# A gated MLP's gate and up projections by seven block products over pairs of token chunks, pairs outermost

## Chip, cores and metric

One core of one Trainium2 chip. The metric is the device time of one execution in microseconds (us). Engines: PE (TensorE matmul), PEld (its weight load), DVE (VectorE), ACT (ScalarE), POOL (GpSimd), SP (SyncE, which here only issues transfers).

## The reference, cut to what the change touches

One layer of a decoder on 2048 tokens of width 1024, in float32: a first projection, four sequence mixers (RWKV, mLSTM, sliding window, "fox" attention with forget gates), an output projection, and a gated MLP with a short convolution. The change is in how the last lines are computed:

```python
x = x + _rmsnorm(y @ w_out[l], norm_mix_post[l])
h = _rmsnorm(x, norm_ffn_pre[l])
gate, up = jnp.split(h @ ffn_w_up[l], 2, axis=-1)     # 1024 -> 2 x 2816
gate = _causal_dwconv(gate, ffn_conv_w[l], ffn_conv_b[l])   # 3 taps over time
f = jax.nn.gelu(gate, approximate=True) * up
x = x + _rmsnorm(f @ ffn_w_down[l], norm_ffn_post[l])
```

## The kernel before, in words

Every large product is made of float16 parts: an operand x becomes hi = float16(x s) and lo = float16(x s - hi) with a power of two s, and a product is three matmuls, hi hi + hi lo + lo hi, into one psum bank.

Stage 1 (RWKV and the windowed mixers) fills the first 1,200 us. Stage 2 runs the fox attention and, between its steps, the **output projection** by tiles of 128 tokens, the "o tiles". `o_front` loads a tile of y, scales it and transposes it by DMA into `yt` (L289); `o_back` multiplies it with the resident `Wo` (L275 to L277: 96 matmuls of 256 columns), norms it, adds x, writes the result to DRAM (`x2`), and `norm_u` puts the normed tile as hi/lo, again through DMA transposes, into `U2`: four resident tiles `V` of 512 tokens each, which the MLP reads. All transposes, and the loads of y and of the weights, go through SP's queue in program order.

Stage 3, `stage_n`, is the MLP (the "mixer"). The 2816 channels are 22 blocks of 128 (j), taken in 11 groups (g) of two. Groups are the outer loop, the four chunks (c) of 512 tokens the inner one. Once per group `split_w` prepares the weights: load to `wst` (L232), absolute maximum per row on DVE (L233), over the partitions on POOL (`partition_all_reduce`, L238), hi on ACT (L252), lo on DVE (L253). Then for each chunk:

```python
for jj in range(GF):                       # two channel blocks
    self.gemm_cm(pg, w, U[c], 0)           # gate: 24 matmuls of 512 columns
    ...gb = [two old columns | gate], 3 taps on DVE (L1489 to L1491), gelu on ACT (L1492)
    self.gemm_cm(pu, w, U[c], P)           # up: 24 matmuls
    f = pu * un * t                        # DVE, L1496
nc.gpsimd.partition_all_reduce(...)        # L1500: one scale for the float16 parts of f
...fh, fl on ACT and DVE (L1507, L1508)
for i in range(NSUB): for n in range(2):   # down: 48 matmuls into psd, acc += on DVE (L1522)
```

In the mixer POOL has only copies and memsets of two columns (L1482, L1484, L1487) and the two reductions (L238, L1500). In the last group each finished tile goes through the last norm: DVE L1531, a POOL addition of 128x1024 (L1532), the write to `out`. Small powers (`rsqrt`) are a POOL tensor_tensor too (L215). The order on each engine is made by a scheduler from the program; pools of one or two buffers set what may run ahead.

Of the kernel before, what the change touches and what calls it, by code (L numbers as in the profile page):

```python
# [31 lines left out]
# ---------------------------------------------------------------- constants of the shapes  # L32
# [65 lines left out]
def _layout(inp):  # L98
    """Only moves the inputs about."""
# [18 lines left out]
    up = a["ffn_w_up"].reshape(KT, P, 2, NF, P).transpose(3, 1, 0, 2, 4)  # L118
# [20 lines left out]
# ---------------------------------------------------------------- the program  # L139
class Trunk:  # L140
# [13 lines left out]
    # ---- set-up  # L154
    def setup(self):
# [16 lines left out]
        # norm gains brought to [-2, 2) by a power of two, which the output's scale undoes  # L172
        self.gsc = cst.tile([P, 2], F32, name="gsc")
        self.ug = cst.tile([P, 2], F32, name="ug")
        for n, k in enumerate(("g1", "g2")):
            m = self.small.tile([P, 1], F32, name="gm")
            nc.vector.tensor_reduce(out=m, in_=self.pc[k], axis=AX.X, op=ALU.max, apply_absolute_value=True)
            mm = self.small.tile([P, 1], F32, name="gmm")
            nc.gpsimd.partition_all_reduce(mm, m, P, RMAX)
            un, sc = self.pow2(mm, 0)  # L180
            nc.vector.tensor_copy(out=self.gsc[:, n:n + 1], in_=sc)
            nc.vector.tensor_scalar(out=self.ug[:, n:n + 1], in0=un, scalar1=2.0 ** -9, scalar2=None, op0=ALU.mult)
# [17 lines left out]
    def pow2(self, m, e):  # L200
        """(un, sc): un = 2**(exponent of m) * 2**-e, sc = 1 / un."""
        nc = self.nc
        o = self.small.tile([P, 3], F32, name="p2")
        nc.vector.tensor_scalar(out=o[:, 0:1], in0=m, scalar1=1e-30, scalar2=2.0 ** -e, op0=ALU.max, op1=ALU.mult)
        nc.vector.tensor_scalar(out=o[:, 1:2].bitcast(I32), in0=o[:, 0:1].bitcast(I32), scalar1=0x7F800000, scalar2=None, op0=ALU.bitwise_and)
        nc.vector.reciprocal(out=o[:, 2:3], in_=o[:, 1:2])
        return o[:, 1:2], o[:, 2:3]

    def rsqrt(self, out, v, mul, eps):
        """out = (v * mul + eps) ** -0.5, on small tiles."""  # L210
# [6 lines left out]
    def sigm(self, e):  # L217
        """e = 1 / (1 + e), by ScalarE's exp and ln."""
# [5 lines left out]
    def split_w(self, pool, tag, srcs, n, ug, bufs=None):  # L224
        """Loads [P, n] weights (given as pieces; with self.twice, again for each use), returns hi, lo (float16) of w * sc and the undoing scale."""
# [31 lines left out]
    def gemm_cm(self, ps, w, u, n0=0, nn=P, step=C):  # L257
        """ps[n, t] = sum_d w[d, n] u[d, t], in steps over t"""
# [10 lines left out]
    def gemm_tm(self, ps, u, sl, w, n0, nn):  # L269
        """ps[t, n] = sum_d u[d, t] w[d, n]"""  # L270
# [8 lines left out]
    def split_t(self, x, sc, h, out):  # L279
        """hi/lo float16 parts of the token tile x * sc (sc per token, or None), channel-major."""  # L280
# [10 lines left out]
    def norm_u(self, pool, x, n, grow, U, i, h=None, bufs=1):  # L291
        """Normalises the token tile x (in place) and puts it channel-major, as hi/lo float16 scaled by 2**9, into slice i of U."""
# [29 lines left out]
    # ---- stage 1: first norm, RWKV-7, and the input projection of the other groups  # L322
    def stage1(self):
# [8 lines left out]
        with ExitStack() as cx:  # L332
# [46 lines left out]
    def rwkv_setup(self, xp):  # L379
# [18 lines left out]
        # block-diagonal tiles with a background of zeros  # L398
# [15 lines left out]
    def rwkv_mix(self, c, j, w, cy):  # L414
        """Channel-major projection j of chunk c with the token shift mixed in, to DRAM."""
# [30 lines left out]
    def rwkv_unit(self, c, hp, half):  # L446
        """Two heads, 256 tokens: four chunks of 64, two token tiles of 128."""
# [21 lines left out]
        # decay  # L469
# [12 lines left out]
        # a  # L482
# [5 lines left out]
        # normalised kk  # L488
# [11 lines left out]
        # scaled forms; bk has (beta, k) for even and (k, beta) for odd chunks  # L500
# [16 lines left out]
        # gate and bonus (with the norm's offset)  # L517
# [21 lines left out]
        # token-major, after M^T: BK = [beta~; k~] (odd chunks the other way round), V opposite to where U will be, alpha^  # L539
# [9 lines left out]
        # M^T, entry [s, t]: rows (beta, k) as in bk, columns (alpha, r)  # L549
# [39 lines left out]
        # merge 16 -> 32; F1, F2 the parts of M between 16-blocks of a 32-block and between 32-blocks; items (h, i)  # L589
# [20 lines left out]
        # X = M_ak V  # L610
# [9 lines left out]
        # [W | U] = T64 [alpha^ | X], T64 = T32 + T32 F2 T32  # L620
# [16 lines left out]
        # chunk operators  # L637
# [18 lines left out]
        # chain of states  # L656
# [13 lines left out]
        # outputs  # L670
# [9 lines left out]
        # per-head layer norm, bonus, gate  # L680
# [15 lines left out]
    # ---- projections of the other groups, to DRAM  # L696
    def fillers(self, ctx):
# [43 lines left out]
        # forgetting attention's queries (negated) and keys as sums of two float32r parts  # L741
# [50 lines left out]
        # values as two float16 parts: head, [hi | lo]. The operands' scales bound the sums by 2**35.  # L792
# [68 lines left out]
    # ---- stage 2: mLSTM, sliding-window and forgetting attention, output projection  # L861
    def stage2(self):
        with ExitStack() as ck, ExitStack() as co:
# [14 lines left out]
            with ExitStack() as cf:  # L878
                self.fox_pools(cf, 5, 6, 8, 4, 2, 4)
                self.u2p = self.pool(self.ctx, "u2", side="right")  # L880
# [4 lines left out]
                for c in range(1, NC):  # L885
                    if c > 1:
                        self.fox(8)
                    if c <= 2:
                        self.o_tiles(c - 1)
            ck.close()  # L890
            u2b = self.pool(self.ctx, "u2b")
            for c in range(2, NC):
                self.U2[c] = u2b.tile([P, 2, KT, C], F16, name=f"V{c}")
            for c in range(2, NC):
                self.o_tiles(c)

    def logsig(self, pool, x, name):
        """log sigmoid of a small tile"""
# [9 lines left out]
    def gates_f(self, kp, psp):  # L908
        """Cumulative sum of the forgetting attention's log gates, as two float32r parts, to DRAM."""
# [29 lines left out]
    def gates_m(self, kp, tp, psp):  # L939
        """All gates of mLSTM at once; blocks of 128 tokens lie on partitions 16 * head + block."""  # L940
# [26 lines left out]
        # the running maximum across the blocks  # L967
# [25 lines left out]
        # token-major: g, weights, exp(-m)  # L993
# [10 lines left out]
        # rows to broadcast by the tensor engine, as two float32r parts below each other  # L1004
# [11 lines left out]
    def gates(self, ctx):  # L1016
        """The gates of mLSTM and of the forgetting attention, the sliding window's bias."""
# [21 lines left out]
    def mlstm_front(self, ib):  # L1039
        """What does not wait for the state: q times exp(a), k with its weights, the decay matrix."""  # L1040
# [10 lines left out]
        # q times exp(a), broadcast over the channels of each head; k token-major with its weights  # L1051
# [9 lines left out]
        # decay matrix exp(a_t + g_s), s <= t  # L1061
# [9 lines left out]
    def mlstm_back(self, ib, q, k, va, so, qi, kw, Dm):  # L1071
# [13 lines left out]
        # state, block-diagonal over the heads  # L1085
# [7 lines left out]
        # h = num / max(|den|, exp(-m)), its norm, output gate  # L1093
# [16 lines left out]
    def swa_bias(self, tp):  # L1110
        """Rows of the relative bias with the window's mask, to DRAM, from where they are read with a shift per partition."""
# [60 lines left out]
            # numerators as two float16 parts, keys on the partitions  # L1172
# [41 lines left out]
    # forgetting attention; its logits, negated, have float32 operands as sums of two float32r parts  # L1214
# [7 lines left out]
    def fox_setup(self):  # L1222
# [9 lines left out]
        # values as two float16 parts: tile of tokens, head, [hi | lo]  # L1232
# [139 lines left out]
    def o_tiles(self, c):  # L1372
        if c == 0:
            self.of = self.o_front(0)
# [191 lines left out]
```

## Time and profile before

| | us |
|---|---|
| median of three runs (lowest, highest) | 3163.35 (3162.02, 3165.93) |
| the profiled execution: span of the instructions | 3156.8 |
| what the median has beyond this span | 6.5 |
| to 1200: stage 1; 1200 to 1640: fox phase with 11 of the 16 o tiles | 1640 |
| 1640 to 1785: the other five o tiles, and the first mixer matmuls | 145 |
| 1785 to 3111: mixer | 1326 |
| 3111 to the end: last norms and writes | 46 |

A row by stretches has the busy time of each engine in that stretch with its count of instructions, then the granted clock of PE (1.00 is 2.4 GHz, 0.5 is 1.2 GHz), the share of the 16 DMA engines and their rate. A timeline row has start, duration, engine, line, operation, tiles and shapes, and in brackets how long the engine was idle before it and what ended that; "issue" stands for nothing that the profile shows.

### The profile page before, as it was taken

What the parts mean: (1) busy time and instruction counts of PE and PEld (TensorE: products, weight loads), DVE (VectorE), ACT (ScalarE), POOL (GpSimd) and SP (SyncE); (2) the same over time, 40 slices, a digit from 0 to 9 for tenths busy, and PEclk for the clock granted to TensorE, in tenths of its full rate; (3) what the DMA queues carried; (4) which work ended last, traced back from release to release, by engine and by line L of the source; (5) the groups of instructions that cost most, each with busy time, mean ns of one, the idle gap of its engine ahead of it and who ended that gap; (6) DMA issues with size and microseconds to landing.
All of it is one profiled execution on the core that took longest, in us unless ns stands there. A gap on an engine that the chain in (4) does not pass through costs nothing. (4 is left out here: it accounts for less than half of the span.)

```text
span 3156.8 us, 45312 instructions
## 1 busy us (share of the span) xinstructions
PE 2793.4 (88%) x17006; PEld 1665.4 (53%) x17006; DVE 1899.9 (60%) x4341; ACT 963.9 (31%) x2004; POOL 586.2 (19%) x943
## 2 busy tenths in 40 slices
PE   1599889898997998787777899999999999999995
PEld 0145577676776876575554444444444444444442
DVE  3474555557775665677765455655655656556565
ACT  2342222335542234566653211211111211111121
POOL 1243222222322332122221100000000000000033
PEclk9799889899997998688888899999999999999998
DMA  6442323244653378999985200100100100001023
GB/s 177 100 111 60 93 57 96 81 104 117 153 137 86 83 196 186 241 213 220 190 194 134 67 27 14 41 14 27 41 14 27 40 13 28 27 14 40 14 99 115
DMA packets 460580, 291.47 MB, mean 92 GB/s; under 512 B 351736, under 2 KB 407416, under 8 KB 460360
## 3 DMA queue, kind: packets, MB, share of 16 engines
q1 hardware_dynamic: 396704, 236.34, 30.1%
q10 hardware_dynamic: 63656, 52.23, 6.1%
q8 instruction: 134, 2.20, 0.3%
q14 instruction: 86, 0.70, 0.1%
HBM read 153.10 MB, written 66.43 MB: 70 GB/s over the span
## 5 line engine op out<-in xcount | busy, mean ns | idle before, releaser
L1522 DVE SCALAR_TENSOR_TENSOR acc<-psd,uns,acc 128x512 f32<-128x512 f32 x320 | 237.0, 749 | 210.9 <-PE psd L1518 209.6
L1516 PE MATMUL psd<-hi_dn,fh 128*128 128x512 f16 x704 | 268.6, 382 | 17.7 <-ACT fh L1507 17.5
L1517 PE MATMUL psd<-lo_dn,fh 128*128 128x512 f16 x704 | 268.8, 382 | 0.0
L265 PE MATMUL psg<-V,hi_up 128*128 128x512 f16 x704 | 267.1, 379 | 0.0
L267 PE MATMUL psg<-V,lo_up 128*128 128x512 f16 x704 | 266.8, 379 | 0.1
L266 PE MATMUL psg<-V,hi_up 128*128 128x512 f16 x704 | 266.8, 379 | 0.0
L265 PE MATMUL psu<-V,hi_up 128*128 128x512 f16 x704 | 266.8, 379 | 0.0
L266 PE MATMUL psu<-V,hi_up 128*128 128x512 f16 x704 | 266.8, 379 | 0.0
L267 PE MATMUL psu<-V,lo_up 128*128 128x512 f16 x704 | 266.8, 379 | 0.0
L1518 PE MATMUL psd<-hi_dn,fl 128*128 128x512 f16 x704 | 261.7, 381 | 0.3
L267 PEld LDWEIGHTS <-lo_up 128*128 128x128 f16 x1408 | 137.8, 98 | 166.3 <-DVE lo_up L253 0.6
L265 PEld LDWEIGHTS <-hi_up 128*128 128x128 f16 x1408 | 137.8, 98 | 165.7
L266 PEld LDWEIGHTS <-hi_up 128*128 128x128 f16 x1408 | 137.8, 98 | 165.6
L275 PE MATMUL psg<-Wo,yt 128*128 128x256 f16 x512 | 149.3, 292 | 54.2 <-DMA yt<-hl 54.2
L1485 ACT ACTIVATE gb<-psg,un_up 128x512 f32<-128x512 f32 x88 | 60.3, 686 | 386.7 <-PE psg L267 386.7
L265 PE MATMUL psg<-U,hi_cm 128*128 128x512 f16 x256 | 104.3, 407 | 70.9 <-ACT hi_cm L252 70.9
L233 DVE TENSOR_REDUCE wm<-wst 128x1 f32<-128x1024 f32 (+1 forms) x91 | 109.6, 1206 | 92.4 <-DMA wst<-in_w_up 51.2
L265 PE MATMUL psf<-U,hi_fm 128*128 128x256 f16 x576 | 162.2, 282 | 1.9 <-DVE zf L745 1.9
L1487 POOL COPY gtail<-gb 128x2 f32<-128x2 f32 x88 | 18.8, 214 | 775.5 <-ACT gb L1485 775.5
L266 PE MATMUL psf<-U,hi_fm 128*128 128x256 f16 x576 | 162.3, 282 | 0.0
L267 PE MATMUL psf<-U,lo_fm 128*128 128x256 f16 x576 | 162.1, 281 | 0.0
L276 PE MATMUL psg<-Wo,yt 128*128 128x256 f16 x512 | 148.9, 291 | 0.0
(423 smaller groups left out, 6291.3 us busy)
## 6 DMA issues: line engine op xcount, KB each, us to landing
wst<-in_w_up SPq DMA_DIRECT2D x44, 512.0 KB
wst<-in_w_dn SPq DMA_DIRECT2D x22, 512.0 KB
zin<-zR SPq DMA_DIRECT2D x80, 128.0 KB
ka<-kA ACTq DMA_DIRECT2D x40, 256.0 KB
wst<-in_w_cm SPq DMA_DIRECT2D x17, 512.0 KB
zR<-m SPq DMA_DIRECT2D x32, 256.0 KB
wso<-in_w_o SPq DMA_DIRECT2D x32, 256.0 KB
xr<-in_x ACTq DMA_DIRECT2D x16, 512.0 KB
```

The lines of the kernel that those rows point to most:

```text
L233: nc.vector.tensor_reduce(out=m[:, i:i + 1], in_=st[:, :w], axis=AX.X, op=ALU.max, apply_absolute_value=True)
L265: nc.tensor.matmul(ps[:, sl], lhsT=hi[:, k, n0:n0 + nn], rhs=uh[:, k, sl], start=k == 0, stop=False)
L266: nc.tensor.matmul(ps[:, sl], lhsT=hi[:, k, n0:n0 + nn], rhs=ul[:, k, sl], start=False, stop=False)
L267: nc.tensor.matmul(ps[:, sl], lhsT=lo[:, k, n0:n0 + nn], rhs=uh[:, k, sl], start=False, stop=k == KT - 1)
L275: nc.tensor.matmul(ps, lhsT=uh[:, k, sl], rhs=hi[:, k, n0:n0 + nn], start=k == 0, stop=False)
L276: nc.tensor.matmul(ps, lhsT=uh[:, k, sl], rhs=lo[:, k, n0:n0 + nn], start=False, stop=False)
L1485: nc.scalar.activation(out=gb[:, 2:], in_=pg, func=AF.Copy, scale=un)
L1487: nc.gpsimd.tensor_copy(out=prev[jj], in_=gb[:, C:C + 2])
L1516: nc.tensor.matmul(ps, lhsT=fh[:, jj, sl], rhs=dh[:, o], start=jj == 0, stop=False)
L1517: nc.tensor.matmul(ps, lhsT=fh[:, jj, sl], rhs=dl[:, o], start=False, stop=False)
L1518: nc.tensor.matmul(ps, lhsT=fl[:, jj, sl], rhs=dh[:, o], start=False, stop=jj == GF - 1)
L1522: nc.vector.scalar_tensor_tensor(out=acc[t][:, ns], in0=ps, scalar=uns, in1=acc[t][:, ns], op0=ALU.mult, op1=ALU.add)
```

## The change

**Products.** Let a pair be two chunks, and split the 1024 inputs of a product into two halves of 512. Gate and up of one block j over a pair are then a 2x2 by 2x2 block product, which is done with seven products instead of eight (Winograd's form). Each has K = 512: 12 matmuls of 512 columns, so 84 per j and pair instead of 96. The operands are sums of weight quarters (three more per j, `S`) and of input quarters (three more, and a fourth as step between). The seven go into three psum banks a, b, c, one buffer each, and are put together by ACT and DVE.

**Order.** Pairs are outermost: pass 0 does all 11 groups for the first pair, pass 1 for the second. In pass 0 the prepared weights (seven quarters hi and lo) are also written to DRAM (`wU`, `wD`), from where pass 1 loads them back.

**Inputs.** An o tile and the one 512 tokens later are combined (`o_combine`), transposed (28 blocks of 128x128 each for hi and lo) and written to DRAM (`u2d`, 7.3 MB per pair); `load_u(p)` brings a pair back in seven loads of 1 MB, once before the second pair's o tiles, and once between the passes.

The core of the diff:

```diff
+    def o_combine(self, p, i, q):
+        tt = lambda o, x, y: nc.vector.tensor_tensor(out=q[:, o], in0=q[:, x], in1=q[:, y], op=ALU.subtract)
+        nc.gpsimd.tensor_tensor(out=q[:, 4], in0=q[:, 1], in1=q[:, 0], op=ALU.subtract)
+        tt(2, 0, 6)
+        tt(3, 1, 2)
+        tt(5, 7, 3)
...
+        nc.scalar.copy(out=h[:, 0], in_=qv)
+        nc.sync.dma_start_transpose(out=ut[:, 0]..., in_=h[:, 0])
+        nc.vector.tensor_tensor(out=h[:, 1], in0=qv, in1=h[:, 0], op=ALU.subtract)
+        nc.sync.dma_start_transpose(out=ut[:, 1]..., in_=h[:, 1])
+        for n in range(2):
+            nc.sync.dma_start(out=dst, in_=ut[:, n])
...
-            for g in range(NG):
-                    Wt.append(self.split_w(self.wp, "up", [a[0], a[1]], 2048, self.ug[:, 1:2], bufs=3))
-                for c in range(NC):
+            for p in range(2):
+                if p:
+                    self.load_u(p)
+                for g in range(NG):
+                    for jj in range(GF):
+                        self.ffn_up(p, j, self.up_weights(p, j), F[:, jj], m[:, jj], prev)
+                    Wd = self.down_weights(p, g, GF)
+                    prev = self.ffn_down(p, g, GF, NG, F, m, Wd, acc)
...
+    def up_weights(self, p, j):
+        if p:
+            nc.sync.dma_start(out=W..., in_=self.wU[j])
+            return W
+        nc.sync.dma_start(out=R..., in_=self.A["w_up"][j])            # L1522, 1 MB
+        nc.vector.tensor_reduce(out=m[:, 0:1], in_=R..., op=ALU.max, apply_absolute_value=True)
+        nc.gpsimd.partition_all_reduce(m[:, 1:2], m[:, 0:1], P, RMAX)  # L1525
+        gt = lambda o, x, y, op: nc.gpsimd.tensor_tensor(out=o, in0=x, in1=y, op=op)   # L1529
+        gt(S[:, 1], R[:, 2], R[:, 0], ALU.subtract)
+        gt(R[:, 0], R[:, 0], R[:, 1], ALU.add)
+        gt(S[:, 0], R[:, 0], R[:, 2], ALU.subtract)
+        gt(S[:, 2], R[:, 3], S[:, 0], ALU.subtract)
+        for o, x in ((slice(0, 4), R), (slice(4, 7), S)):
+            nc.scalar.activation(out=W[:, 0, o], in_=x, func=AF.Copy, scale=sc)
+            nc.vector.scalar_tensor_tensor(out=W[:, 1, o], in0=x, scalar=sc, in1=W[:, 0, o], op0=ALU.mult, op1=ALU.subtract)
+        nc.sync.dma_start(out=self.wU[j], in_=W...)
...
+    def ffn_up(self, p, j, W, F, m, filler):
+        product(a, 2, 5, True, False)          # 12 matmuls each, then next(filler): one psd tile of the group before
+        nc.scalar.activation(out=X, in_=a, func=AF.Copy, scale=un)
+        product(b, 4, 2, True, False)
+        add(g2, b, X)
+        product(a, 3, 6, False, True)
+        product(b, 5, 3, False, False)
+        product(c, 0, 1, True, False)
+        product(b, 1, 4, False, True)
+        product(c, 6, 0, False, True)
...
+        nc.gpsimd.tensor_tensor(out=t, in0=t, in1=up..., op=ALU.mult)  # L1607, 128x1024
+    def ffn_down(...):
+        nc.gpsimd.partition_all_reduce(mm[:, 2:4], mm[:, 0:2], P, RMAX)  # L1615
...
+                elif t % 2 and n:
+                    nc.scalar.activation(out=tmp, in_=ps, func=AF.Copy, scale=us)
+                    nc.gpsimd.tensor_tensor(out=acc[t][:, ns], in0=tmp, in1=acc[t][:, ns], op=ALU.add)  # L1639
```

The taps now run on both chunks at once (1024 columns), one on ACT and two on DVE. `down_weights` is like `split_w` (reduction at L1552) with a write to `wD` in pass 0, a load in pass 1. The last norm (`ffn_out`, L1650 to L1658) is as before, with its tile of x in the pool of the raw weights (two buffers). The other hunks of the diff drop comments and renumber lines.

**POOL, steady mixer.** First a stretch of the kernel before (`gtail` and `gb`: the two columns carried between chunks; `wmm`, `fm`: the maxima of weights and of f); a row "ISA" that names tiles is a reduction:

```order
L238 ISA wmm<-wm 128x1
L1484 COPY gb<-gtail 128x2
L1487 COPY gtail<-gb 128x2
L1484 COPY gb<-gtail 128x2
L1500 ISA fm<-fm 128x1
```

Then one half of a group in pass 0 of the changed kernel. A bare "ISA" row, without tiles, is an instruction that sets up POOL's code for the row behind it:

```order
L1525 ISA
L1525 ISA wm<-wm 128x1
L1529 ISA
L1529 TENSOR_TENSOR raw<-raw 128x512
L1615 ISA
L1615 ISA fmm<-fmm 128x2
L1529 ISA
L1529 TENSOR_TENSOR S<-raw 128x512
L1529 TENSOR_TENSOR S<-raw,S 128x512
L1525 ISA
L1525 ISA wm<-wm 128x1
L1601 COPY tails<-gb 128x2
```

Additions and reductions now alternate; the steady mixer had no bare row before. In pass 0 there are 83 of them, in pass 1 there are 21; the whole program has 150 against 62.

**SP, from the last o tiles to the first weights.** Before, the loads of weights (`wst`) stand between the transposes of the last o tiles:

```order
L289 DMA_TRANSPOSE V_17300<-hl 128x8x128 x2
L1408 DMA y<-ybuf 128x1024
L232 DMA wst<-in_w_up 128x1024 x2
L289 DMA_TRANSPOSE yt<-hl 128x8x128 x2
L232 DMA wst<-in_w_dn 128x1024 x2
```

Now the last tiles run through to the writes of `u2d`, and the first weights come behind them:

```order
L290 DMA_TRANSPOSE yt<-hl 128x8x128 x4
L1401 DMA_TRANSPOSE ut<-h_18142 128x28x128
L1403 DMA_TRANSPOSE ut<-h_18142 128x28x128
L1406 DMA u2d_13756<-ut 896x1x512 x2
L1401 DMA_TRANSPOSE ut<-h_18406 128x28x128
L1403 DMA_TRANSPOSE ut<-h_18406 128x28x128
L1406 DMA u2d_13756<-ut 896x1x512 x2
L1522 DMA raw<-in_w_up 128x2048 x2
L1548 DMA rawd<-in_w_dn 128x1024 x2
```

Of the 16 o tiles, nine now lie in the fox phase and seven behind it. On PE no mixer matmul stands before the last o tile's.

## Rows read from the trace of the kernel before

**Rows 1.** the page of the profile: its first line
```profile
span 3156.8 us, 45312 instructions
```

**Rows 2.** busy time by stretch: us, then each engine, granted clock, DMA share, GB/s
```profile
1200.00:1640.00 440.00, 341.79 (x2333) 264.95 (x2331) 297.81 (x732) 256.37 (x620) 103.62 (x94) 0.83 0.99 208
1640.00:1785.00 145.00, 102.65 (x661) 68.63 (x662) 72.00 (x124) 45.53 (x69) 23.86 (x28) 0.83 0.51 129
1785.00:3111.00 1326.00, 1319.28 (x6099) 595.42 (x6097) 802.57 (x1340) 244.35 (x336) 104.30 (x260) 1.00 0.10 32
3111.00:3157.00 46.00, 15.62 (x60) 6.06 (x57) 20.64 (x28) 6.56 (x11) 16.61 (x12) 0.70 0.33 116
2000.00:2500.00 500.00, 499.78 (x2315) 225.86 (x2313) 300.76 (x510) 89.40 (x120) 25.76 (x92) 1.00 0.08 26
```

**Rows 3.** timeline of POOL in the steady mixer
```profile
1955.49 0.35 POOL L1500 PARTITION_ALL_REDUCE fm<-fm  x1 [3.79 <-DVE fm L1499]
```

**Rows 4.** timeline of POOL near the end, where additions and reductions alternate
```profile
3043.94 0.19 POOL L1484 COPY gb<-gtail 128x2 f32<-128x2 f32 x1 [0.68 <-DVE gc L1491]
3050.82 0.38 POOL L1500 PARTITION_ALL_REDUCE fm<-fm  x1 [6.70 <-issue]
...
3060.97 0.59 POOL L215 TENSOR_TENSOR nss<-rsq,mhalf 128x1 f32<-128x1 f32 x1 [6.94 <-issue]
```

**Rows 5.** what POOL waited for: us in total, times, longest us
```profile
POOL fm L1500 <- DVE fm L1499: 142.5, 39, 4.9
POOL wmm L238 <- issue: 135.8, 22, 8.9
...
POOL ss L215 <- issue: 43.8, 6, 8.5
...
POOL m L427 <- issue: 21.2, 3, 7.3
```

**Rows 6.** costliest groups by form: busy us, mean ns of one, idle before
```profile
L1532 POOL TENSOR_TENSOR wst<-wst,acc 128x1024 f32<-128x1024 f32 x16 | 41.5, 2591 | 15.3 <-issue 5.2 <-DVE acc L1531 5.1 <-DVE rsq L214 4.0
...
L427 POOL TENSOR_TENSOR m<-z 128x512 f32<-128x512 f32 x32 | 35.2, 1102 | 21.2 <-issue 21.2
```

**Rows 7.** DMA, 1300 to 1640 us: kinds and issues by line
```profile
q1 hardware_dynamic: 159572, 47.52, 77.1%
...
fPt<-fhl SPq DMA_TRANSPOSE x120
...
yt<-hl SPq DMA_TRANSPOSE x20
V<-hl SPq DMA_TRANSPOSE x19
```

**Rows 8.** timeline of PE where the fox phase ends
```profile
1637.47 0.66 PE L1323 MATMUL pso<-c,fot 128*128 128x64 f32 x4 [0.46 <-ACT fot L1320]
1645.57 0.40 PE L275 MATMUL psg<-Wo,yt 128*128 128x256 f16 x1 [7.44 <-DMA yt<-hl]
```

**Rows 9.** tile yt, 1638 to 1785 us: output-projection matmuls, first and last start
```profile
L277 PE MATMUL psg<-Wo,yt x160: 272/273/421, 1646.9 to 1775.3; 128*128 128x256 f16 x160
```

**Rows 10.** tile psu, 1638 to 1785 us: up-projection matmuls beside them
```profile
1638.00:1785.00 147.00, 16.52 (x72) 2.23 (x3) 0.83 0.51 130
```

**Rows 11.** timeline of DVE behind the last output-projection tile
```profile
1777.04 0.16 DVE L1435 TENSOR_TENSOR oss<-oss 128x1 f32<-128x1 f32 x1 [8.74 <-ACT psg L1433]
...
1787.51 1.23 DVE L284 TENSOR_TENSOR hl<-xr,hl 128x1024 f16<-128x1024 f32 x1 [1.17 <-ACT hl L283]
```

**Rows 12.** the chain that ended last, its tail
```profile
3118.00 4.77 issue
3122.78 0.39 POOL fm L1500
...
3143.64 2.89 DMA out<-wst
3146.59 3.99 DMA wst<-x2buf
```

More of the change, by code (lines that the diff above doesn't have):

```diff
@@ L884, in stage2, with load_u @@
                 self.fox(3)
[L885 to L889, printed above, removed]
-            ck.close()
[L891 to L895, printed above, removed]
+                self.o_pairs(0, range(0, 2))
+                self.fox(8)
+                self.o_pairs(0, range(2, 4))
+                self.fox(8)
+            ck.close()
+            self.u2p = self.pool(self.ctx, "u2")
+            self.U2 = [self.u2p.tile([P, NSUB, 2, 4, P], F16, name=f"V{n}") for n in range(7)]
+            self.load_u(0)
+            self.o_pairs(1, range(4))
+    def load_u(self, p):
+        for n in (5, 2, 6, 3, 1, 4, 0):
+            self.nc.sync.dma_start(out=self.U2[n].rearrange("p i h k t -> p (i h k t)"), in_=self.u2d[p][:, n])
     def logsig(self, pool, x, name):
@@ L1355, in o_setup @@
         nc = self.nc
-        self.U2 = [self.u2p.tile([P, 2, KT, C], F16, name=f"V{c}") for c in range(2)] + [None] * (NC - 2)
+        self.u2d = [self.dram.tile([P, 7, NSUB * 2 * 4 * P], F16, name=f"u2d{p}") for p in range(2)]
         self.so = self.small = self.pool(ctx, "small_o", bufs=2, side="right")
@@ L1458, in stage_n @@
[L1458 to L1473 removed]
+            self.sn = self.small = self.pool(ctx, "small_n", bufs=4)
@@ new lines, in ffn_up, with product, add @@
+    def ffn_up(self, p, j, W, F, m, filler):
+        nc, wk, U = self.nc, self.wk, self.U2
+        un = self.unu[:, j:j + 1]
+        fw = lambda n: self.pc["fw"][:, 3 * j + n:3 * j + n + 1]
+        bank = lambda n: self.psw.tile([P, C], F32, name=f"ps{n}")
+        def product(ps, w, u, first, last):
+            for k in range(4):
+                ks = slice(k * P, (k + 1) * P)
+                for n, (a, b) in enumerate(((0, 0), (0, 1), (1, 0))):
+                    nc.tensor.matmul(ps, lhsT=W[:, a, w, ks], rhs=U[u][:, :, b, k], start=first and k == 0 and n == 0, stop=k == 3 and n == 2, skip_group_check=True)
+            next(filler, None)
+        def add(out, ps, x):
+            nc.vector.scalar_tensor_tensor(out=out, in0=ps, scalar=un, in1=x, op0=ALU.mult, op1=ALU.add)
+        gb = wk.tile([P, 2 * C + 2], F32, name="gb")
+        up = wk.tile([P, 2, C], F32, name="up")
+        X = wk.tile([P, C], F32, name="X")
+        g2 = gb[:, C + 2:]
+        if p == 0:
+            nc.gpsimd.memset(gb[:, 0:2], 0.0)
+        else:
+            nc.gpsimd.tensor_copy(out=gb[:, 0:2], in_=self.tails[:, j])
+        a, b, c = bank("a"), bank("b"), bank("c")
+        product(a, 2, 5, True, False)
[3 more added lines that the diff above has]
+        product(a, 3, 6, False, True)
+        nc.scalar.activation(out=gb[:, 2:C + 2], in_=a, func=AF.Copy, scale=un)
+        product(b, 5, 3, False, False)
+        add(up[:, 1], b, X)
+        product(c, 0, 1, True, False)
+        add(up[:, 1], c, up[:, 1])
+        product(b, 1, 4, False, True)
+        add(up[:, 0], b, X)
+        product(c, 6, 0, False, True)
+        add(g2, c, g2)
+        if p == 0:
+            nc.gpsimd.tensor_copy(out=self.tails[:, j], in_=gb[:, 2 * C:])
+        t = F.rearrange("p c n -> p (c n)")
+        nc.scalar.activation(out=t, in_=gb[:, 2:], func=AF.Identity, scale=fw(2), bias=self.pc["fb"][:, j:j + 1])
+        nc.vector.scalar_tensor_tensor(out=t, in0=gb[:, 1:2 * C + 1], scalar=fw(1), in1=t, op0=ALU.mult, op1=ALU.add)
+        nc.vector.scalar_tensor_tensor(out=t, in0=gb[:, 0:2 * C], scalar=fw(0), in1=t, op0=ALU.mult, op1=ALU.add)
+        nc.scalar.activation(out=t, in_=t, func=AF.Gelu_apprx_tanh)
+        nc.gpsimd.tensor_tensor(out=t, in0=t, in1=up.rearrange("p c n -> p (c n)"), op=ALU.mult)
+        nc.vector.tensor_reduce(out=m, in_=F, axis=AX.X, op=ALU.max, apply_absolute_value=True)
@@ new lines, in ffn_out @@
+    def ffn_out(self, t, o):
+        nc, small = self.nc, self.sn
+        r = slice(t * P, (t + 1) * P)
+        x = self.raw.tile([P, D], F32, name="xo", tag="raw")
+        nc.sync.dma_start(out=x, in_=self.x2[r])
+        jk = self.wk.tile([P, D], BF16, name="njunk", tag="tmp")
+        ss = small.tile([P, 2], F32, name="nss")
+        nc.scalar.activation(out=jk, in_=o, func=AF.Square, accum_out=ss[:, 0:1])
+        self.small = small
+        self.rsqrt(ss[:, 1:2], ss[:, 0:1], 1.0 / D, EPS)
+        nc.vector.scalar_tensor_tensor(out=o, in0=o, scalar=ss[:, 1:2], in1=self.pr["post2"], op0=ALU.mult, op1=ALU.mult)
+        nc.gpsimd.tensor_tensor(out=x, in0=x, in1=o, op=ALU.add)
+        nc.sync.dma_start(out=self.out[r], in_=x)
@@ L1542, in run @@
         if "N" in self.phases:
-            if "2" not in self.phases:
-                self.u2p = self.pool(self.ctx, "u2")
-                self.U2 = [self.u2p.tile([P, 2, KT, C], F16, name=f"V{c}") for c in range(NC)]
-                for c in range(NC):
-                    self.nc.sync.dma_start(out=self.U2[c], in_=self.pre_u[c])
             self.stage_n()
```

206 lines of the change are left out of this document (111 added, 95 removed).

## The prediction

> **What bounds the kernel now.** I read the stretches first, then who waits for whom in each. In the mixer (1785 to 3111 us) PE is busy 1319.3 of 1326 us at granted clock 1.00 [rows 2]: PE is the bound there and nothing else matters. Its matmul price comes from 2000 to 2500: 499.8 us for 2315 matmuls of 512 columns, 0.216 each. VectorE has 0.61 of that stretch and POOL only 0.08. In the fox phase (1200 to 1640) the DMA engines are the bound, share 0.99, with PE at 0.78 [rows 2]; three quarters of the DMA time is one kind of transfer, of which the transposes are the many [rows 7]. Between 1640 and 1785 nothing is full: there the o tiles run as a chain through transposes, norms and one tile's matmuls, and mixer matmuls fill the gaps. So removed matmuls pay only if PE stays the bound of the mixer, and the question for each part is what it loads on POOL and on SP's queue.
>
> **PE.** Gate and up lose 12 of 96 matmuls per block and pair: 22 x 2 x 12 = 528 of 6336, or 114 us at 0.216. A pass then has 22 x 84 + 11 x 96 = 2904 matmuls, 627 us. That is the whole gain.
>
> **Pass 0, by POOL's own sum.** The order listing of the change has 83 bare rows on POOL there. What one costs is seen where additions and reductions alternate near the end of the kernel before: a reduction waits 6.70 us and the next power 6.94, both for nothing that the profile shows [rows 4], while the steady mixer's reduction waits 3.79, for VectorE [rows 3]. The groups agree: reductions 135.8 / 22 = 6.2 each, additions 21.2 / 3 = 7.1, powers 43.8 / 6 = 7.3 [rows 5]. In a POOL that is behind, these gaps are not hidden by anything. Sum for pass 0: 41 loads before reductions at 6.2 = 254; 42 before additions at 7.1 = 298; 88 weight sums of 512 columns at 1.1 [rows 6] = 97; 36 additions to the accumulators at 1.1 = 40; 22 products of 1024 columns at 2.4 (2.6 is the mean of their like [rows 6], 2.36 the undisturbed ones) = 53; 44 reductions at 0.35 and 45 small copies at 0.19 [rows 3, 4] = 24. That is 766, or about 70 per group, where PE needs 57. Once per group POOL also waits for the maximum of f from VectorE, 142.5 / 39 = 3.7 us a time before [rows 5]: 11 x 3.7 = 40. I take **806 us** for pass 0, with 745 (loads partly under waits) and 850 (more waits) as its ends. Loads would have to cost under about 4.6 us each, (640 - 214 - 40) / 83, for PE to set the pace again. VectorE does not get there: it has the same combining per chunk, half of its 802.6 us [rows 2] per pass, and some 45 us for the larger split.
>
> The Trainium skill (GPSIMD Engine Reference, section 2.1 Instruction dispatch) says that the first call of a freshly loaded POOL kernel pays a load of about 6 us (5.95 measured) that no instruction in the profile shows. The trace agrees in kind, with 6.2 to 7.3. By the page's figure the loads of pass 0 would be an estimated 494 us in place of 552, and the total about 3,340; the sum goes by the rows.
>
> **Pass 1.** Two loads per group, one reduction, two products and four additions: about 25 us of POOL in 57 of PE, so PE paces. Weights come from DRAM, 1.8 MB per block, 5 us at the 350 GB/s that 116 at share 0.33 makes [rows 2], beside 28 us of matmuls. Where a group ends, the scale of f goes VectorE, POOL (with its load), VectorE, ACT, while PE has 60 products' matmuls (13 us) and 24 of down (5 us) left over: 18 us against a chain of 17 to 20. I take 2 us of gap per group, and 10 at the boundary of the passes for the load of the second pair: 627 + 20 + 10 = **657** (632 to 690).
>
> **Fox phase.** Nine o tiles and four combinations in place of eleven tiles: 16 more transposed blocks. 159 transposes of up to eight blocks [rows 7] took 0.77 of 340 us, so about 0.2 per block: 3 us. Writes of `u2d` are 7.3 MB, against 3 MB that two o tiles fewer save; 4.3 MB is 12 us at 350 GB/s, and three times that if pieces of 1 KB are so much dearer. I take 27, since this phase has DMA share 0.99 and hides nothing: **+30** (15 to 50), with the writes waiting on SP ahead of fox transposes inside that.
>
> **From the end of the fox phase to the first weights.** First matmul of an o tile 8 us after the last fox matmul, as before [rows 8]. Load of the first pair ahead of the next tile's transposes on SP: 7.3 MB, 21 us and 4 for the way. Tiles: five took 128.4 us [rows 9], 25.7 each, with 16.5 us of up matmuls between [rows 10] and as many of gate by the listing, 6.6 per tile; that leaves 19, and I take 20 for the combinations: six intervals are 120. Then the last tile: matmuls 10.4 (96 x 0.108), norm 13 (last matmul to the end of VectorE's split at 1788.7 [rows 11]), combination 10 (two subtractions in a row, 3584 columns on ACT and on VectorE at 1.1 us per 1024), transposes of 56 blocks partly beside it 8, first weights 5: 46. Together 8 + 25 + 120 + 46 = **199** (154, if tiles and loads overlap, to 250).
>
> **Tail.** Now the tail is 46 us [rows 2], with 4.77 us of one load, and a write of 2.89 and a load of x of 3.99 in series [rows 12]. After the last products come 120 matmuls of down and eight tiles, of which two share 9.3 us by those rows: **64** (55 to 70).
>
> **Sum.** Fox ends at 1638 [rows 8]. 1638 + 30 + 199 + 806 + 657 + 64 = 3394 against a span of 3156.8 [rows 1]; the median of the runs is 6.5 above the span of the profiled one, so about **3400 us**. The 114 us from PE come off; they are lost because pass 0 runs 180 us longer than its PE work, the mixer can't start under the o tiles, and those tiles now come alone.
>
> **Rivals.**
> *Loads hidden.* POOL's set-up might run under its waits, so that PE paces pass 0 at 640. For it: in the kernel before many reductions show VectorE as their only releaser [rows 5]. Against: those had idle time around them, and POOL here has none. That alone gives 3400 - 166 = 3234, slower still. Only with the front at its low ends as well (overlapping tiles and loads, -45 and -15) and the tail at 55 is it 3165: no change. It decides at 4.6 us per load. Chance 0.07, with a range of 3110 to 3235.
> *A ring of waits.* Engines run in order. POOL waits for f's maximum, f for the last of seven products, the products for a weight buffer (two) whose sums wait on POOL behind that same reduction. If that ring closes in each group, POOL's 70 us and some 15 of PE and ACT add up instead of overlapping: 11 x 85 = 935, total 3530, range 3480 to 3620. For it: one buffer for the sums `S`, and reductions that stand between the sums of the next block in the order. Against: raw weights have two buffers, and POOL is a whole block ahead. Chance 0.13.
> *The change does not do what it says in the products.* With one buffer per bank, PE may wait for each eviction: a, b and c are each reused, some 0.7 us for ACT or VectorE at two places per block, 31 us per pass, inside the pass 0 that POOL sets but not in pass 1: 3430 to 3450. Chance 0.06, inside the range.
>
> **How the numbers follow.** The forecast has 0.74. Its ends: the bounds of pass 0 (-61, +44), the front (-45, +51), fox (-15, +20), pass 1 (-25, +33) and the tail will not all fall on one side; pass 0 and the front both low give 3294, both high 3495. I take 3290 to 3500, which leaves out the hidden loads and most of the ring. About 0.2% is what a measurement of this kernel can tell from no change. Faster by more: 0.04, half of the first rival and little else. Within: 0.03. Slower: 0.93.
>
> **What would show it right or wrong.** In the profile after: 528 fewer matmuls of 512 columns; POOL at 0.9 of pass 0, idle, where it shows as idle, with "issue" before reductions and sums, 6 to 7 us a time; PE at 0.75 in pass 0 and over 0.95 in pass 1; some 200 us between the last fox matmul and the first product with PE at about a half, and the granted clock below 1.00 there. Wrong if PE is over 0.9 busy in pass 0 (loads hidden), if POOL waits there mostly for VectorE or PE (the ring), or if the front is under 150 us.

## The result: 3,543 us, slower by 12%, outside the range

Median 3542.61 us of four runs (3541.28 to 3552.69) against 3164.64 us for the kernel before on the same chip; ratio 1.1185, 95% interval 1.1156 to 1.1214. The direction was forecast, the size was not: 3,400 was said, 3,500 was the upper end. The profile after, by its page and by the stretches that answer to [rows 2] (the same columns: us, PE, PEld, DVE, ACT, POOL, granted clock, DMA share, GB/s):

```profile
span 3541.0 us, 44277 instructions
```

```profile
1668.00:1883.00 215.00, 92.76 (x676) 72.84 (x675) 73.42 (x107) 49.15 (x68) 36.24 (x30) 0.68 0.67 176
1883.00:2809.00 926.00, 648.58 (x2663) 276.19 (x2664) 457.46 (x547) 218.71 (x208) 248.04 (x219) 0.84 0.24 94
2842.00:3470.00 628.00, 622.30 (x2872) 280.50 (x2871) 296.62 (x383) 147.03 (x180) 139.03 (x110) 1.00 0.26 92
3470.00:3541.00 71.00, 28.88 (x123) 12.19 (x121) 34.00 (x42) 17.00 (x25) 36.84 (x24) 0.73 0.30 104
```

The bounds of these stretches are single rows: the last fox matmul, the first product, and the load of prepared weights with which pass 1 starts. They stand in the timeline of PE, in the rows of tile Wup (transfer issues and products), and here are the three that give the cuts:

```profile
1667.81 0.66 PE L1325 MATMUL pso<-c,fot 128*128 128x64 f32 x4 [0.46 <-ACT fot L1322]
```

```profile
L1571 PE MATMUL psa<-V,Wup x1056: 377/380/635, 1883.5 to 3454.6; 128*128 128x512 f16 x176
...
L1519 SPq DMA_DIRECT2D Wup<-wU x22: 319/320/424, 2809.4 to 3413.6; - x22
```

| term of the sum | forecast | measured | off by |
|---|---|---|---|
| end of the fox phase | 1638 + 30 | 1668.5 | 0 |
| from there to the first product | 199 | 215 | +16 |
| pass 0 | 806 | 926 | **+120** |
| pass 1 and tail | 657 + 64 = 721 | 732 | +11 |
| span | 3394 | 3541.0 | +147 |

The second row is what is called the front below. Its forecast ended with the landing of the first raw weights. They landed at 1865.9, 17.5 us ahead of the first product; between the two lie the first maximum, a reduction and a sum on POOL with a set-up of its code ahead of each (4.4 and 6.6 us), and ACT's split. Cut where the forecast cut it, the front took 197 us, right within 2, and pass 0 took 943, 137 over.

In pass 0 PE is busy 0.70 of the time, with a granted clock of 0.84 and matmuls that therefore take longer each; in pass 1 it is busy 0.99 at 1.00, as in the mixer before [rows 2]. So the question is pass 0. What POOL waited for there (us in total, times, longest):

```profile
POOL wm L1525 <- issue: 125.7, 20, 8.9
POOL S L1529 <- issue: 83.4, 12, 7.1
POOL tails L1601 <- DVE gb L1575: 74.2, 17, 16.1
POOL wm L1552 <- issue: 66.2, 11, 6.2
POOL acc L1639 <- issue: 65.0, 9, 7.7
POOL raw L1529 <- issue: 62.8, 9, 7.4
POOL fmm L1615 <- issue: 53.7, 9, 6.2
POOL acc L1639 <- DVE Wup L1536: 34.3, 5, 7.0
POOL acc L1639 <- ACT tmp L1638: 33.1, 9, 4.3
```

The six rows with "issue" are the set-ups: 457 us in 70 gaps, 6.1 before a reduction and 7.0 before an addition, as priced from [rows 4, 5]; the other 13 set-ups lie in gaps that end with an operand. POOL's work is 248 us. What is left, some 210 us, are gaps that end with an operand of VectorE, ACT or a load (the three longest rows of these stand here, 142 us). VectorE in its turn waited 315 us for the results of POOL's reductions:

```profile
DVE p L205 <- POOL wm L1525: 139.4, 20, 12.9
DVE p L205 <- POOL fmm L1615: 105.2, 9, 14.7
DVE p L205 <- POOL wm L1552: 70.2, 11, 13.8
```

Now the chain that ended last, one lap of a steady group:

```profile
2311.70 1.22 DVE fm L1608
...
2313.58 5.45 issue
2319.03 0.39 POOL wm L1552
...
2320.57 0.67 DVE up L1575
...
2321.28 4.44 PE psb L1571 x12
2325.72 2.60 PE psc L1571 x12
...
2328.34 2.01 ACT Wup L1535
...
2330.38 2.35 DVE Wup L1536
...
2342.98 2.36 POOL F L1607
...
2346.60 4.55 issue
2351.15 0.38 POOL wm L1525
...
2351.60 7.18 issue
```

The lap goes POOL, VectorE, a set-up (5.45), a reduction on POOL, VectorE, 7 us of PE, ACT, VectorE, POOL, a set-up (4.55), a reduction, a set-up (7.18), and so on. The same reduction comes again 89.8 us later. Of this lap the chain puts 35.5 us to set-ups, 18 to POOL's work, 20 to VectorE's, 7 to PE's and 5 to ACT's. (The rows between, and those of the second half of the lap, are of the same kinds.)

### The profile page after: what moved, and what is told of

Same layout as the page of the kernel before. It is cut to its first block, busy times and chain, and to the rows that moved or that the text cites. A ratio compares the mean times of both kernels' runs of the same rounds, so it can differ in the third digit from the quotient of the medians.

```text
span 3541.0 us, 44277 instructions
## 1 busy us (share of the span) xinstructions
PE 2768.6 (78%) x16478; PEld 1635.2 (46%) x16478; DVE 1881.1 (53%) x3926; ACT 1101.3 (31%) x2053; POOL 912.6 (26%) x1031
## 5 line engine op out<-in xcount | busy, mean ns | idle before, releaser
L1571 PEld LDWEIGHTS <-Wup 128*128 128x128 f16 x3696 | 376.0, 102 | 781.7 <-issue 311.5
L1571 PE MATMUL psb<-V,Wup 128*128 128x512 f16 x1584 | 417.7, 418 | 215.1 <-DVE up L1575 132.4
L1632 PE MATMUL psd<-Wdn,fh 128*128 128x512 f16 x2112 | 495.3, 385 | 59.4 <-ACT fh L1622 44.9
L1632 PEld LDWEIGHTS <-fh 128*128 128x128 f16 x2112 | 207.9, 99 | 318.2 <-ACT fh L1622 48.4
L1571 PE MATMUL psa<-V,Wup 128*128 128x512 f16 x1056 | 249.2, 386 | 66.2 <-ACT Wup L1535 55.4
L1571 PE MATMUL psc<-V,Wup 128*128 128x512 f16 x1056 | 252.1, 385 | 10.3 <-DVE p L206 9.1
L1639 POOL TENSOR_TENSOR acc<-tmp,acc 128x512 f32<-128x512 f32 x80 | 118.6, 1482 | 384.3 <-ACT tmp L1638 285.1
L276 PE MATMUL psg<-Wo,yt 128*128 128x256 f16 x512 | 152.2, 298 | 66.0 <-DMA yt<-hl 65.3
L278 PE MATMUL psg<-Wo,yt 128*128 128x256 f16 x512 | 148.9, 295 | 16.0 <-DMA yt<-hl 16.0
L277 PE MATMUL psg<-Wo,yt 128*128 128x256 f16 x512 | 152.2, 298 | 0.0
L276 PE MATMUL psf<-hi_fv,U 128*128 128x256 f16 (+1 forms) x512 | 137.5, 275 | 1.5 <-ACT zc L778 1.5
L278 PE MATMUL psf<-hi_fv,U 128*128 128x256 f16 (+1 forms) x512 | 137.4, 274 | 0.0
L277 PE MATMUL psf<-lo_fv,U 128*128 128x256 f16 (+1 forms) x512 | 137.3, 274 | 0.0
```

Of the source, the lines that this page charges most:

```text
L276: nc.tensor.matmul(ps, lhsT=uh[:, k, sl], rhs=hi[:, k, n0:n0 + nn], start=k == 0, stop=False)
L277: nc.tensor.matmul(ps, lhsT=uh[:, k, sl], rhs=lo[:, k, n0:n0 + nn], start=False, stop=False)
L278: nc.tensor.matmul(ps, lhsT=ul[:, k, sl], rhs=hi[:, k, n0:n0 + nn], start=False, stop=k == KT - 1)
L1571: nc.tensor.matmul(ps, lhsT=W[:, a, w, ks], rhs=U[u][:, :, b, k], start=first and k == 0 and n == 0, stop=k == 3 and n == 2, skip_group_ch ...
L1632: nc.tensor.matmul(ps, lhsT=fh[:, a, jj, c, sl], rhs=Wd[:, b, jj, ns], start=jj == 0 and k == 0, stop=jj == GF - 1 and k == 2)
L1639: nc.gpsimd.tensor_tensor(out=acc[t][:, ns], in0=tmp, in1=acc[t][:, ns], op=ALU.add)
```

## The experiments

Each was timed beside runs of the kernel before on the same chip, and ratios are to those. Stages are cut as above. The theory under test at first: **A**, POOL's set-ups pace pass 0; its rival **B**, single psum banks and VectorE's queue pace it, whatever POOL does.

### Additions off POOL (dve_all)

```diff
-        gt = lambda o, x, y, op: nc.gpsimd.tensor_tensor(out=o, in0=x, in1=y, op=op)
+        gt = lambda o, x, y, op: nc.vector.tensor_tensor(out=o, in0=x, in1=y, op=op)
...
-        nc.gpsimd.tensor_tensor(out=t, in0=t, in1=up..., op=ALU.mult)
+        nc.vector.tensor_tensor(out=t, in0=t, in1=up..., op=ALU.mult)
...
-                    nc.gpsimd.tensor_tensor(out=acc[t][:, ns], in0=tmp, in1=acc[t][:, ns], op=ALU.add)
+                    nc.vector.tensor_tensor(out=acc[t][:, ns], in0=tmp, in1=acc[t][:, ns], op=ALU.add)
```

> All additions and products of the mixer that stood on POOL (weight sums, f's product, a quarter of the accumulator additions) go to VectorE, so that POOL keeps only reductions and small copies, and bare rows fall from 150 to 48. Theory A (POOL's code set-up, about 6.5 us each, paces pass 0, directly and through VectorE, which waits for the reductions): pass 0 falls from 922 us (84 per group) to 640-690, total 3260-3310. Theory B (single psum banks and VectorE's in-order queue pace it, whatever POOL does): VectorE gets some 15 us more per group, pass 0 stays at 850-950, total 3470-3560.

Measured 3266.2 us, ratio 1.0297 (1.0238 to 1.0357). Pass 0 took 668 us (1876 to 2544), and no gap of POOL there ends with "issue". Its stretch has DVE 0.79 busy and PE 0.90:

```profile
1876.00:2544.00 668.00, 604.16 (x2665) 266.35 (x2666) 528.97 (x679) 221.56 (x208) 39.63 (x81) 0.95 0.34 130
```

A holds and B doesn't: VectorE took 70 us more and pass 0 lost 258. The reductions are all still on POOL, and without additions between them none shows a set-up.

### Reductions of the weights left out (no_wred)

```diff
-        nc.gpsimd.partition_all_reduce(m[:, 1:2], m[:, 0:1], P, RMAX)
-        un, sc = self.pow2(m[:, 1:2], 12)
+        un, sc = self.pow2(m[:, 0:1], 12)
```

and the same in `down_weights`: these reductions are left out, not moved.

> The reductions of the weights' maxima over the partitions are left out (each partition is scaled by its own maximum, so the numbers computed are others); POOL keeps all its additions and the one reduction of f per group; bare rows 150 to 88, two per group. Theory A: pass 0 640-690, total 3260-3310, as where the additions were moved. Theory B: pass 0 over 850, total 3470-3560. If A holds here and not where additions went to VectorE, VectorE's load is what is left.

Measured 3258.9 us, ratio 1.0274 (1.0213 to 1.0335); pass 0 took 652. All of the additions are back on POOL, which works as long as in the change, and the time is that of the run before:

```profile
1869.00:2521.00 652.00, 599.54 (x2665) 265.26 (x2664) 468.59 (x547) 219.40 (x207) 249.27 (x187) 0.96 0.34 133
```

So it is neither the additions nor the reductions, but that they alternate. Nor is it POOL's work beside VectorE's, which is all there again.

### Only the weight sums off POOL (dve_sums)

The first of the three edits above, alone.

> Only the weight sums go to VectorE; bare rows 150 to 124, about 5 per group in pass 0 in place of 7.5. Theory A: POOL has 34 us of set-ups and 10 of work per group, under PE's 57, but each reduction that VectorE waits for still comes 6 us late: pass 0 660-760, total 3280-3380. Theory B: 850-950, total 3470-3560.

Measured 3432.5 us, ratio 1.0821 (1.0756 to 1.0887); pass 0 took 808, above what A gave and below B. POOL is now far from full, with 123 us of work and 241 of visible set-ups in 36 gaps. Another 18 changes between the two kinds lie in gaps that end with an operand; at 6.6 each, an estimate, POOL is taken for some 480 of the 808 us.

```profile
1884.00:2692.00 808.00, 628.35 (x2642) 270.71 (x2643) 492.41 (x622) 219.91 (x206) 123.07 (x133) 0.88 0.28 108
```

```profile
POOL F L1607 <- issue: 125.8, 17, 9.7
...
POOL wm L1552 <- issue: 42.0, 7, 6.1
POOL fmm L1615 <- issue: 40.8, 7, 5.9
```

And still the chain runs through its set-ups. In the lap shown here the reduction stands 4.30 us behind the product of f, and only then come VectorE's scale, the combination queued behind it, and PE:

```profile
2373.94 2.34 POOL F L1607
...
2376.31 1.23 DVE fm L1608
...
2377.74 4.30 issue
2382.03 0.38 POOL fmm L1615
...
2382.81 0.66 DVE up L1575
...
2383.51 5.19 PE psb L1571 x12
```

Over the whole of pass 0 "issue" has 17.7% of the chain, 143 us, against 2.7% (18 us) in dve_all and 40.9% (379 us) in the change; pass 0 is 140 us longer than in dve_all. VectorE's larger load is not the reason, since dve_all gives it more still. This is the run that tells a sum from a ring: a set-up costs by standing between two engines that wait for each other in order, even where POOL has time to spare.

### An eighth product, in the change and with POOL free (eight, eight_dve)

```diff
         product(c, 0, 1, True, False)
+        product(c, 2, 3, False, False)
```

> An eighth product of 12 matmuls is added per block and pair (its operands are those of another product, so the numbers computed are others); 528 matmuls more, 57 us of PE per pass, all else as in the change. Theory A (POOL's set-ups pace pass 0): PE's slack of 24 us per group takes the five of them in pass 0, which grows by 0-25; pass 1 grows by 57; total 3600-3625. Theory B (PE is in the ring at every step): both passes grow, total 3650-3660.

Measured 3611.4 us, ratio 1.1385 (1.1321 to 1.1450). Pass 0 took 933 us (+7), the rest 68 more: the first stretch below is pass 0, the second the most of pass 1.

```profile
1876.00:2809.00 933.00, 683.95 (x2929) 296.88 (x2930) 473.53 (x549) 221.43 (x208) 252.14 (x220) 0.86 0.24 93
2842.00:3540.00 698.00, 683.42 (x3158) 307.86 (x3157) 311.27 (x388) 147.70 (x181) 134.94 (x111) 1.00 0.22 84
```

The matmuls that the change saves in pass 0 are worth 7 us there, of the 57 that PE has less to do, as A has it.

> The version with all additions on VectorE (3266 us), with the eighth product added as before (528 matmuls more; the operands are those of another product, so the numbers computed are others). If PE paces both passes there, each grows by 57 and the total is 3370-3385; if pass 0 still has slack of its own, 3325-3350. It is also what seven products save against eight in the same frame.

Measured 3305.3 us, ratio 1.0416 (1.0363 to 1.0469), only 39 above the same frame with seven, and below both forecasts. Pass 0 took 648 us, 20 less than with seven products; the rest grew by 54. The same stretch of pass 0, with eight products and with seven (dve_all):

```profile
1900.00:2480.00 580.00, 573.84 (x2649) 259.48 (x2648) 481.99 (x626) 199.67 (x189) 27.95 (x76) 1.00 0.33 130
```

```profile
1900.00:2480.00 580.00, 522.92 (x2304) 230.39 (x2304) 460.56 (x602) 192.25 (x181) 33.75 (x73) 0.95 0.33 126
```

With eight, PE is busy 0.99 of the stretch at a granted clock of 1.00; with seven, 0.90 at 0.95. So even with POOL free, seven products saved nothing in pass 0: what PE no longer had to do showed as waits, in dve_all 31 us of them until ACT had emptied bank a.

```profile
PE psa L1571 <- ACT gb L1591: 31.3, 8, 5.3
```

### Single waits taken from the ring (bank2, tails_act)

```diff
-        bank = lambda n: self.psw.tile([P, C], F32, name=f"ps{n}")
+        bank = lambda n: self.psw.tile([P, C], F32, name=f"ps{n}", bufs=2 if n == "b" else 1)
```

> The change with one edit: psum bank b has two buffers (all eight banks are then used), so that PE's next product into b needn't wait for VectorE's combination, which stands behind POOL's reductions on VectorE's queue. In the change PE waits 132 + 42 us so in pass 0. Theory C (a ring POOL, VectorE, PE, VectorE, POOL adds some 11 us per group to POOL's own 73): pass 0 falls from 932 to 830-890, total 3440-3500. Theory D (the other waits come from POOL's own queue, PE's place in it doesn't matter): pass 0 stays at 915-940, total 3525-3550.

Measured 3550.8 us, ratio 1.1184 (1.1148 to 1.1220); pass 0 took 923. PE's wait for VectorE went from 132 us (first row, from the change) to 18, and another took its place. D holds, and C doesn't:

```profile
PE psb L1571 <- DVE up L1575: 132.1, 15, 17.3
```

```profile
PE psd L1632 <- ACT fh L1622: 172.7, 9, 33.8
...
PE psb L1571 <- DVE up L1575: 17.9, 8, 15.4
```

```diff
-            nc.gpsimd.tensor_copy(out=self.tails[:, j], in_=gb[:, 2 * C:])
+            nc.scalar.copy(out=self.tails[:, j], in_=gb[:, 2 * C:])
```

> The change with one edit: the copy of the two last columns (22 in pass 0) goes to ACT; POOL waited 74 us in pass 0 for VectorE ahead of it. Set-ups stay (150 bare rows). Theory E (POOL's waits for single operands add to its own sum, 778 us by the trace, up to the 926 of pass 0): without this wait pass 0 is 850-890, total 3470-3510. Theory F (a ring of POOL and VectorE, in which a wait removed at one place comes back at the next): pass 0 stays at 910-935, total 3525-3555.

Measured 3539.2 us, ratio 1.1153 (1.1096 to 1.1210); pass 0 took 915, so 11 of the 74 us. The next operand's wait grew from 33 to 95:

```profile
POOL acc L1639 <- ACT tmp L1638: 94.9, 15, 14.0
```

F holds, and E doesn't: a wait that is removed at one place comes back at the next.

### The front (dve_u2dact, dve_raw)

Both on top of the version with additions on VectorE.

```diff
-            nc.sync.dma_start(out=dst, in_=ut[:, n])
+            nc.scalar.dma_start(out=dst, in_=ut[:, n])
```

> On top of the version with all additions on VectorE (3266 us): the writes of u2d go out on ACT's queue, so that SP's transposes for the fox phase and for the next o tiles don't stand behind a write that waits for its transposes. If SP's waits made the fox phase 30 us and the front 60 us longer, the fox phase ends 15-25 us earlier and the total is 3220-3250; if the DMA engines' bandwidth did, or ACT now stands in the same wait, 3260-3290.

Measured 3318.6 us, ratio 1.0454 (1.0429 to 1.0478), 52 worse and outside both ranges. ACT now stands where SP stood, with the o tiles' work behind it: once it waits 22.8 us for a transpose ahead of a write. The front took 236 us against 205, and the last fox matmul starts at 1684.7 against 1671.4:

```profile
ACT o L1469 <- DMA ut<-h: 22.8, 1, 22.8
```

```diff
+            self.raw = self.pool(self.ctx, "raw_n", bufs=2)
+            self.first = []
+            for j in range(2):
+                R = self.raw.tile([P, 4, C], F32, name="raw", tag="raw")
+                self.nc.scalar.dma_start(out=R..., in_=self.A["w_up"][j])
+                self.first.append(R)
             self.load_u(0)
...
+        if self.first:
+            R = self.first.pop(0)
```

> On top of the version with all additions on VectorE (3266 us): the first two blocks' raw weights are loaded on ACT's queue before the second pair's o tiles, in place of behind them on SP. Their load (8.4 us) and first maximum (2.3) leave the chain between the last o tile and the first product, and VectorE can form the sums there: total 3250-3258. No gain if the split to float16 stays behind the o tiles' work on ACT and VectorE for another reason: 3266.

Measured 3216.9 us, ratio 1.0131 (1.0106 to 1.0157): 49 us gained where 8 to 16 were expected. The front went from 205 to 174 us (1674.1 to 1848.3), and pass 0 from 668 to 642, with a granted clock of 0.99 against 0.95 in its steady part. Why the steady part gained too was not tried apart.

### What else holds pass 0, and the tail (raw_a2, raw_sqrt)

Both on top of dve_raw.

```diff
-        bank = lambda n: self.psw.tile([P, C], F32, name=f"ps{n}")
+        bank = lambda n: self.psw.tile([P, C], F32, name=f"ps{n}", bufs=2 if n == "a" else 1)
```

> The version with additions on VectorE and early raw weights (3217 us), with two buffers for psum bank a: PE waited 31 us in pass 0 for ACT to empty a, and with an eighth product it had no gaps. If the single bank is what keeps pass 0 above its PE work, pass 0 falls from 649 by 20-45 and the total is 3170-3200; if VectorE (0.8 busy in pass 0) is, the gap moves to b and c: 3210-3225.

Measured 3214.8 us, ratio 1.0151 (1.0105 to 1.0196): no gain, pass 0 641. The waits for a are gone and stand at b, and a little at c, for VectorE, which is busy 0.84 of the steady part:

```profile
PE psb L1579 <- DVE up L1583: 15.4, 11, 1.7
PE psb L1579 <- DVE gb L1583: 14.6, 9, 4.5
```

```diff
-        self.rsqrt(ss[:, 1:2], ss[:, 0:1], 1.0 / D, EPS)
+        nc.vector.tensor_scalar(out=ss[:, 0:1], in0=ss[:, 0:1], scalar1=1.0 / D, scalar2=EPS, op0=ALU.mult, op1=ALU.add)
+        nc.scalar.activation(out=ss[:, 0:1], in_=ss[:, 0:1], func=AF.Sqrt)
+        nc.vector.reciprocal(out=ss[:, 1:2], in_=ss[:, 0:1])
...
-        nc.gpsimd.tensor_tensor(out=x, in0=x, in1=o, op=ALU.add)
+        nc.vector.tensor_tensor(out=x, in0=x, in1=o, op=ALU.add)
```

> The version with all additions on VectorE and the first raw weights loaded early (3217 us), with the last norm as in the run where it gained 22 us in the kernel before: square root on ACT, reciprocal and addition on VectorE. Bare rows 48 to 47. The last eight tiles lose at most a set-up or two and POOL's 2.4 us additions: 3195-3212. Still above the kernel before, since the fox phase (+30), the front and the tail stay.

Measured 3221.3 us, ratio 1.0143 (1.0101 to 1.0186): no gain, where 5 to 22 us were expected. In this frame no reduction stands between the last powers, so there was next to nothing to remove.

### The lesson applied to the kernel before (before_sqrt, sqrt_o, sqrt_all)

The same last-norm edit in the kernel before; then the same in the o tiles behind the fox phase; then in all 16.

> The kernel before, with the last norm's power done by a square root on ACT and a reciprocal on VectorE, and its addition on VectorE: POOL has no additions in the last group, so the four reductions of f and the powers there don't alternate, bare rows 62 to 55. If set-ups on POOL cost their 4.6 to 7 us on the chain there (7 of them, 4 to 5 on the path), the end comes 15-25 us earlier, 3140-3150 against 3163; if ACT's own table changes between square root and gelu (8 in all) or VectorE's 1.2 us per addition take that back, no difference.

Measured 3152.9 us beside 3175.0, ratio 0.9928 (0.9911 to 0.9945).

```diff
+        self.acts = t >= 11
         self.rsqrt(t1[:, 2:3], ss[:, 2:3], 1.0 / D, EPS)
...
-        nc.gpsimd.tensor_tensor(out=x, in0=x, in1=o, op=ALU.add)
+        (nc.vector if t >= 11 else nc.gpsimd).tensor_tensor(out=x, in0=x, in1=o, op=ALU.add)
...
+        if self.acts:
+            nc.scalar.activation(out=t[:, :n], in_=t[:, :n], func=AF.Sqrt)
+            nc.vector.reciprocal(out=out, in_=t[:, :n])
```

> The kernel before with the last norm's power on ACT (3153 against 3175), and in the five o tiles behind the fox phase too: powers by ACT's square root and VectorE's reciprocal, the addition of x on VectorE, so that POOL there has only the weights' reductions; bare rows 55 to 45. If set-ups lie on the o tiles' chain (two powers per tile behind a reduction, 6 to 7 us where idle), 10-30 us less than 3153; if DMA transposes and loads set their rhythm, or ACT's table changes cost as much, the same within 8 us.

Measured 3118.1 us beside 3174.3, ratio 0.9826 (0.9796 to 0.9856): 35 us below before_sqrt, a little more than the 10 to 30 expected. The last of the five tiles' matmuls now starts at 1750.0 in place of 1775.3 [rows 9], 25 us earlier, with PE at 0.85 of the stretch and POOL with 7 us of work:

```profile
L281 PE MATMUL psg<-Wo,yt x160: 272/273/421, 1650.7 to 1750.0; 128*128 128x256 f16 x160
```

```profile
1640.00:1760.00 120.00, 102.50 (x696) 68.76 (x695) 77.09 (x142) 58.24 (x89) 6.77 (x15) 0.94 0.65 163
```

> The kernel before with powers by ACT and x added on VectorE in all 16 o tiles (3118 us where it was done in the last five). If the fox phase is bound by the DMA engines, its eleven tiles gain nothing, and table changes on ACT may cost: 3115-3140. If POOL's set-ups held fox steps too, below 3110.

Measured 3114.4 us, ratio 0.9829 (0.9792 to 0.9866): no more than sqrt_o. In the eleven tiles inside the fox phase, where the DMA engines are busy 0.99 of the time [rows 2], the edit is worth nothing. Both versions beat both kernels.

## Why the prediction was wrong

**Right: the direction, PE's saving, the price and the number of set-ups, four of five terms.** PE's saving is real and comes in pass 1, where the eighth product costs 54 and 68 us (eight_dve, eight, tail included; 57 was worked out). The fox phase (+30) came as said, to the microsecond by luck: in runs with the same code up to there its last matmul starts anywhere between 1665.4 (eight) and 1686.7 (tails_act). The front, cut where the forecast cut it, was right within 2 us; pass 1 and the tail were 11 short. POOL's set-ups cost what [rows 5] gave, 6.1 and 7.0 us, and there were 83. Without the alternation pass 0 is 652 or 668, near the 640 named as PE's pace.

**Wrong: the step "Once per group POOL also waits for the maximum of f ... 11 x 3.7 = 40".** It took POOL's time in pass 0 as its own sum with one short wait. The wait that it named did not even show: all nine gaps seen ahead of f's reduction end with "issue". And it gave POOL no idle time but this ("POOL here has none", in the rival on hidden loads). Of the 120 us that pass 0 went over, some 34 are POOL's own work (248 against 214; weight sums took 1.3 us at the median and up to 3.0, not 1.1), the set-ups came out about as summed, and most of the rest is waits for operands: not 40 but roughly 125, when the 210 us of such gaps are lessened by the 13 set-ups that lie in them (13 x 6.6 = 86, at most). POOL, VectorE and ACT wait for each other in order, each set-up holds VectorE's queue with the combinations that stand behind the scale, and what VectorE is late with comes back to POOL. dve_sums shows it best, with POOL taken for some three fifths of pass 0 and pass 0 still 808.

**The rival that came nearest.** "A ring of waits" had 0.13 and 3530, and its 935 us for pass 0 lie close to the 926. That is partly luck, for its path was only partly right: it was put down to the weight buffers and PE's products, and PE has 7 us of a lap; bank2 shows that the bank it doubled is no link that decides. The ring is POOL and VectorE, with ACT's splits. The sign that the prediction set for it did not come either: POOL's idle time in pass 0 ends with "issue" for 457 of some 667 us, and not mostly with VectorE or PE. It is VectorE's 315 us of waits for reductions, and dve_sums, that show the ring. The rival should have had more weight: the order listing showed reductions whose results VectorE needs between sums that POOL needs VectorE for, and the "POOL is a whole block ahead" that spoke against it was not read from any row.

**A page's figure.** The Trainium skill (GPSIMD Engine Reference, section 2.1 Instruction dispatch) has a load of about 6 us (5.95) on the first call of freshly loaded code. The trace agrees, with 6.1 before a reduction and 7.0 before an addition, and shows it at each change between the two. By the page's figure the forecast would have been an estimated 60 us lower, and further off.

**What stays open.** Why the early raw weights also sped up the steady part of pass 0 (clock 0.99 against 0.95) and how much seven products would save there if VectorE had less to do.

## What to carry to other kernels

Don't take an engine that answers to others by its own sum alone: here a fixed cost on it counted where another engine's in-order queue stood behind its answer, even when the engine was not full (dve_sums). On POOL, count the changes between kinds of operation (additions or powers, and reductions over partitions), not the operations: taking either kind away was worth about the same here (668 and 652 us). And before saving matmuls, ask what else in the loop will be next: with POOL free, PE stood waiting for ACT, with that wait gone for VectorE (raw_a2), and the seven products' saving in pass 0 was not to be had.

## What had not been expected of the hardware

That a change of POOL's code is paid again at each alternation, for hundreds of microseconds in a steady loop (457 us in 70 gaps), and that in the kernel before taking away the few that it had in five o tiles and the last group, with the additions and powers beside them, gained 56 us of 3,174, though POOL was busy 19% of the span. ACT's way round, with 17 table changes of 1.28 us, 13 of them in these rows, was cheaper:

```profile
L1498 ACT ACT_TABLE_LOAD x8 | 10.3, 1283 | 1.3 <-DVE gc L1497 1.2
...
L216 ACT ACT_TABLE_LOAD x5 | 6.4, 1283 | 0.1
```
